# A hybrid RWKV-7 and MoBA layer: alternating the two halves of the array in small products, with TensorE in program order

## The chip, the cores and the metric

The kernel runs on one core of one Trainium2 chip. The metric is device time in microseconds (us) of one execution. Before the change the median of three runs is 842.22 us (840.99 to 842.25). All durations below come from one profiled execution of that kernel.

## The reference, cut to what matters

One decoder layer on 256 tokens of width 2048, in float32. The input is normalised, one product with `w_in` (2048 x 12416) feeds two token mixers and their gates, each mixer's result goes through a projection of its own, the two are merged by gates, and `w_out` closes the layer:

```
h = rms_norm(x, norm_w);  p = h @ w_in
y_a = rwkv7_mix(p_r, p_k, p_v, p_wd, p_ad, ...) * silu(z_a)
y_b = moba_attention(p_q, p_kq, p_vq, q_norm_w, k_norm_w) * silu(z_b)
merged = sigmoid(g_a) * (y_a @ w_proj_rwkv) + sigmoid(g_b) * (y_b @ w_proj_moba)
out = x + merged @ w_out
```

Both mixers have 16 heads of 64 features. The RWKV mixer is a recurrence over the tokens, which the kernel computes in blocks of 64 tokens: it needs the products of all keys with all queries of a block, an inverse of a triangular matrix of 32 x 32, and a state carried from block to block. With 256 tokens and blocks of 256 the MoBA mixer is plain causal attention: logits, softmax, values.

## The kernel before, in words

**Jobs.** The large products are cut into chunks of 512 columns (`chunk`, L240), and each chunk into jobs: half of a 1 MB load of weights, which ACT and DVE split into a high and a low part (`split_hi` L211, line 216; `split_lo` L218, line 222), so that three fast products stand for one exact one. A job is 24 matmuls of 256 columns (`mm_fm`, line 329) or 12 of 512 columns (`mm_tm`, lines 347 to 349). There are 258 jobs, numbered from 0. `run_jobs` (L253) emits `prep(i)`, the split of job i, then `run(i - 2)`: the matmuls of the job two before, the work on a finished chunk (`post`), and `pump()`. The parts of a split have three buffers each.

**Side work.** Everything else is written as generators. `pump()` (L199) takes one step of each generator in `urgent` and one step of the first one in `queue`; a step ends at a `yield`. A step may hold TensorE, DVE, ACT and GpSimd instructions. A stretch of side work on TensorE between two jobs is called a visit here. `drain(mark)` (L203) takes steps, one after the other, until a named generator is through; `with_need("m0", ...)` and `with_need("v1", ...)` (L1027, L1040) call it ahead of a chunk's post.

The features are handled in two groups of 512 (g = 0, 1), and in a tile of 128 partitions two heads lie one above the other (p = 0 in partitions 0 to 63, p = 1 in 64 to 127). For each group the steps are, in order:
- `rwkv_elem` (L405): low-rank products (lines 430, 431) into two PSUM tiles `pw` and `pa`, each read by ACT sigmoids (lines 432, 435); norms of the keys (line 467, ACT line 469, DVE lines 470 to 473, transposes at line 481).
- `rwkv_r` (L511): the key products, line 533, for each of 4 feature tiles `fi` and each half p a PSUM tile with 4 products of 64 x 128 by 64 x 128, then DVE line 536.
- `rwkv_mid` (L659): the inverse on DVE (lines 564, 567) alongside transposes (lines 620, 643), then a trip through DRAM (lines 571, 576) and the products at lines 593 and 601.
- `rwkv_v` (L680): twelve steps over 4 blocks: lines 670 and 677, ACT line 690; line 694, ACT line 697; line 704. These products already alternate p = 0, p = 1.
- `moba` (L808): six units, for p = 0 then p = 1 one unit u = 0 (4 heads, 128 queries by 128 keys) and two units u = 1, 2 (2 heads, 128 by 256). `logits` (lines 825, 831) is followed by DVE lines 836 to 839 and ACT exponentials (line 843); `normal` by DVE lines 848, 849; `turn` transposes four tiles (line 858) and ACT copies them; `pv` (lines 874, 876) multiplies by the values for one p at a time.
- Group norms (`group_norm`, L720, transposes at line 748) and the transposes of q and k (`qk_post`, L760, line 775, after DVE line 793) run as urgent generators.

**What sets the order.** The program is written with Tile and its scheduler (`schedule_with_timeline_sim=True`). Inside `tc.manual_schedule(engines=...)` the engines named keep the order in which the program emits their instructions; elsewhere the scheduler orders each engine's instructions by its own timing model, the earlier emitted ones first among those that it finds ready. Before the change only the start is ordered by hand (L294: jobs 0 to 3, on DVE, ACT and PE). From job 6 on (L306) all engines are ordered by the scheduler. The root mean square of x (`rms_x`, L158) is emitted in that second loop ahead of job 4: DVE line 159, ACT line 160, DVE line 161, then two TensorE transposes (line 164).

An f32 matmul appears in the trace as two MATMUL records, an f32r one (the main products) and a transpose as one.

Of the kernel before, what the change touches and what calls it, by code (L numbers as in the profile page):

```python
# [13 lines left out]
AF = mybir.ActivationFunctionType  # L14
# [22 lines left out]
def tile_hybrid_block(ctx: ExitStack, tc: tile.TileContext, x, pv, wdu, wau,  # L37
# [17 lines left out]
    def T(tag, shape, dt=F32, bufs=1):  # L55
        return sb.tile(shape, dt, tag=tag, name=nm(tag), bufs=bufs)
# [4 lines left out]
    def PSS():  # L61
        return psd.tile([P, 512], F32, tag="ps", name=nm("ps"))
# [95 lines left out]
    def rms_x():  # L158
        dve.tensor_reduce(rsx, ssx, AX.X, ALU.add)
        act.activation(rsx, rsx, AF.Sqrt, bias=epsr, scale=1.0 / D)  # L160
        dve.reciprocal(rsx, rsx)
        pt = PSS()
        for t in range(2):
            pe.transpose(pt[:, t * P:(t + 1) * P], rsx[:, t:t + 1].to_broadcast([P, P]), ident)
        dve.tensor_copy(rbc, pt[:, 0:S])
# [87 lines left out]
    def run_jobs(look):  # L253
        n = len(jobs)
        emitted = [0]

        def ensure(j):
            while emitted[0] <= j and emitted[0] < len(loads):
                emit_load(emitted[0])
                emitted[0] += 1  # L260

        def prep(i):
            jb = jobs[i]
            ensure(jb["ld"] + 1)
            jb["raw"] = loads[jb["ld"]]["raw"]
            if i >= KT // 2:
                split_hi(jb)
                split_lo(jb)
            elif i:
                split_hi(jb)  # L270
                scale_hi(i, 0)
                scale_hi(i, 1)
                split_lo(jb)
                scale_lo(i, 0)
                scale_lo(i, 1)
            else:
                for u in range(2):
                    split_hi(jb, u)
                    scale_hi(0, u)
                    split_lo(jb, u)  # L280
                    scale_lo(0, u)

        def run(i):
            jb = jobs[i]
            if jb["first"] and jb["pre"]:
                jb["pre"]()
            jb["mm"](jb)
            if jb["end"]:
                jb["post"](jb["st"])
            pump()  # L290


        wt = PSS()
        with tc.manual_schedule(engines=ordered):  # L294
            for _ in range(8):
                pe.transpose(wt[:, 0:P], ident, ident)
            for j, i, turns, sqs in ((None, 0, (0, 1), ()), (None, 1, (), ()), (0, 2, (2, 3), ()),
                                     (1, 3, (), ((0, 0), (1, 0))), (2, 4, (4, 5), ((0, 1), (1, 1))),
                                     (3, 5, (6, 7), ())):
                if j is not None:  # L300
                    run(j)
                turn_x(*turns)
                prep(i)
                for a in sqs:
                    square_x(*a)
        for i in range(6, n + look):  # L306
            if i < n:
                prep(i)
            if i == 6:
                rms_x()  # L310
            if i >= look:
                run(i - look)

    def mm_fm(mh, ml):
        def f(jb):
# [195 lines left out]
    def rwkv_r(g):  # L511
# [14 lines left out]
        r["rr"] = (rh, rl)  # L526
        yield
        for fi in range(4):
            for p in range(2):
                ps = PSS()  # L530
                sl = slice(64 * p, 64 * p + 64)
                for c in range(4):
                    pe.matmul(ps[:, c * P:(c + 1) * P],  # L533
                              bk[sl, fi, c].rearrange("p a t -> p (a t)"),
                              ar[sl, fi, c].rearrange("p a t -> p (a t)"), start=True, stop=True)
                dve.copy_predicated(
                    LL[p][:, fi].rearrange("p c a t -> p c (a t)"),
                    m2.rearrange("p a t -> p (a t)").rearrange("p (o t) -> p o t", o=1)
                    .to_broadcast([P, 4, P]),
                    ps.rearrange("p (c t) -> p c t", c=4))  # L540
            yield
        G = T("sg", [64, 32, 32])
        gd = dp.tile([4, 4, 4, 32, 32], F32, tag="gd", name=nm("gd"))
# [263 lines left out]

    def moba(g):  # L808
        q, k, v = M[g]["q"], M[g]["k"], M[g]["v"]
        s1 = T("cs", [P, 2, 2, S])  # L810
        smt = [T("sg", [P, 4, P]), s1[:, 0], s1[:, 1]]
        for ap in (smt[0], s1):
            pool.memset(ap, -1e30)
        yield
        us = [dict(p=p, u=u, nh=2 if u else 4, nk=S if u else P, sm=smt[u])
              for p in range(2) for u in range(3)]
        pts = {}
        prs = T("bk", [P, 4, 512])

        def logits(n, w):  # L820
            rows = slice(64 * w["p"], 64 * w["p"] + 64)
            ps = PSS()
            if w["u"] == 0:
                for fi in range(4):
                    pe.matmul(ps[:, fi * P:(fi + 1) * P], q[rows, fi, 0:P], k[rows, fi, 0:P],  # L825
                              start=True, stop=True)
                mask = mq[:, 1:2, :].to_broadcast([P, 4, P])
            else:
                for i in range(2):
                    fi = 2 * (w["u"] - 1) + i  # L830
                    pe.matmul(ps[:, i * S:(i + 1) * S], q[rows, fi, P:S], k[rows, fi, :],  # L831
                              start=True, stop=True)
                mask = mq.rearrange("p a t -> p (a t)").rearrange(
                    "p (o t) -> p o t", o=1).to_broadcast([P, 2, S])
            nh, nk, sm = w["nh"], w["nk"], w["sm"]
            dve.copy_predicated(sm, mask, ps.rearrange("p (f t) -> p f t", f=nh))
            mx = T("mx", [P, 4], bufs=2)
            dve.tensor_reduce(mx[:, 0:nh], sm, AX.X, ALU.max)
            dve.tensor_scalar(mx[:, 0:nh], mx[:, 0:nh], -0.125, None, ALU.mult)
            w["Pr"] = prs[:, n % 4, :].rearrange("p (a b) -> p a b", a=nh)  # L840
            w["sum"] = T("smx", [P, 4], bufs=2)
            for i in range(nh):
                act.activation(w["Pr"][:, i, :], sm[:, i, :], AF.Exp, scale=0.125,
                               bias=mx[:, i:i + 1], accum_out=w["sum"][:, i:i + 1])

        def normal(w):
            nh, nk = w["nh"], w["nk"]
            dve.reciprocal(w["sum"][:, 0:nh], w["sum"][:, 0:nh])
            dve.tensor_tensor(w["Pr"], w["Pr"], w["sum"][:, 0:nh].rearrange(
                "p (h o) -> p h o", o=1).to_broadcast([P, nh, nk]), ALU.mult)  # L850

        def turn(w):
            if w["u"] == 0:
                pts[w["p"]] = T("ar", [P, 4, 3, P])
            pt = pts[w["p"]]
            ps = PSS()
            for i in range(4):
                pe.transpose(ps[:, i * P:(i + 1) * P],  # L858
                             w["Pr"].rearrange("p a b -> p (a b)")[:, i * P:(i + 1) * P], ident)
            if w["u"] == 0:  # L860
                act.activation(pt[:, :, 0, :], ps.rearrange("p (f t) -> p f t", f=4), AF.Copy)
            else:
                f0 = 2 * (w["u"] - 1)
                act.activation(pt[:, f0:f0 + 2, 1:3, :],  # L864
                               ps.rearrange("p (f b t) -> p f b t", f=2, b=2), AF.Copy)

        def pv(p):
            rows = slice(64 * p, 64 * p + 64)
            pt = pts[p]
            po = [PSS() for _ in range(2)]  # L870
            for fi in range(4):
                o = po[fi // 2][rows, (fi % 2) * S:(fi % 2 + 1) * S]
                col = slice(fi * P + 64 * p, fi * P + 64 * p + 64)
                pe.matmul(o, v[:, 0, col], pt[:, fi, 0:2, :].rearrange("p a t -> p (a t)"),  # L874
                          start=True, stop=True, skip_group_check=True)
                pe.matmul(o[:, P:S], v[:, 1, col], pt[:, fi, 2, :], start=False, stop=True,
                          skip_group_check=True)
            for half in range(2):
                act.activation(oT[rows, 4 * g + 2 * half:4 * g + 2 * half + 2, :].rearrange(
                    "p f t -> p (f t)"), po[half][rows, :], AF.Copy)  # L880

        for n in range(9):
            if n in (5, 8):
                pv(0 if n == 5 else 1)
            if 2 <= n < 8:
                turn(us[n - 2])
            if 1 <= n < 7:
                normal(us[n - 1])
            if n < 6:
                logits(n, us[n])  # L890
            yield


# [153 lines left out]
        chunk(w_out, 512 * i, 512, KT, out_mm(cuts, out_done(i, sx)), lambda st: None,  # L1047
              pre=out_pre(i, sx))
    run_jobs(2)
    drain()  # L1050


_W = ["w_in", "w_proj_rwkv", "w_proj_moba", "w_out"]
# [39 lines left out]
```

## Time and profile before

| | |
|---|---|
| median of 3 runs | 842.22 us |
| profiled execution, its own time | 843.0 us |
| its span in the trace | 841.3 us |
| TensorE (PE) busy | 832.2 us, 99% |
| DVE busy | 554.3 us, 66% |
| ACT busy | 422.2 us, 50% |
| MATMUL records | 6738 |

The page of the profile gives busy times by engine and the chain of work that ended last. Matmuls are pipelined and their ends are modelled, so a record's duration is longer than the distance to the next; the number of records in a stretch says more than the share that is busy. A row of the timeline holds start, duration, engine, line, operation, tiles, shape and count; neighbours of one kind are merged.

### The profile page before, as it was taken

What the parts mean: (1) busy time and instruction counts of PE and PEld (TensorE: products, weight loads), DVE (VectorE), ACT (ScalarE), POOL (GpSimd) and SP (SyncE); (2) the same over time, 40 slices, a digit from 0 to 9 for tenths busy, and PEclk for the clock granted to TensorE, in tenths of its full rate; (3) what the DMA queues carried; (4) which work ended last, traced back from release to release, by engine and by line L of the source; (5) the groups of instructions that cost most, each with busy time, mean ns of one, the idle gap of its engine ahead of it and who ended that gap; (6) DMA issues with size and microseconds to landing.
All of it is one profiled execution on the core that took longest, in us unless ns stands there. A gap on an engine that the chain in (4) does not pass through costs nothing.

```text
span 841.3 us, 15850 instructions
## 1 busy us (share of the span) xinstructions
PE 832.2 (99%) x6738; PEld 771.0 (92%) x6738; DVE 554.3 (66%) x776; ACT 422.2 (50%) x568; POOL 29.0 (3%) x42
## 2 busy tenths in 40 slices
PE   8999999999999999999999999999999999999998
PEld 7999878899998788899999988999999999998887
DVE  5869958956569569749974579554455566664553
ACT  6785435444437585435444477544444444443342
POOL 5001100000000002000000000000000000000000
PEclk9999999999999999999999999999999999999999
DMA  8564555564434344646564323555656655556772
GB/s 302 176 195 156 178 160 164 179 196 152 136 117 151 110 141 150 195 139 195 199 204 147 106 97 121 191 188 187 195 197 201 198 164 190 198 167 213 231 245 98
DMA packets 83206, 145.78 MB, mean 173 GB/s; under 512 B 11568, under 2 KB 13872, under 8 KB 83136
## 3 DMA queue, kind: packets, MB, share of 16 engines
q1 hardware_dynamic: 71584, 138.55, 50.7%
q10 hardware_dynamic: 11520, 6.16, 2.7%
q8 instruction: 53, 0.87, 0.4%
q14 instruction: 17, 0.14, 0.0%
q0 software_dynamic: 32, 0.05, 0.0%
HBM read 141.61 MB, written 3.15 MB: 172 GB/s over the span
## 4 chain that ended last, share of the span: by engine, by line
PE 98%; DVE 1%; DMA 1%; issue 0%; SPq 0%; ACT 0%
PE pm L329 59%; PE pm L348 9%; PE pm L347 9%; PE pm L349 9%; PE ps L533 2%; PE ps L670 1%; PE ps L831 1%; PE ps L874 1%; PE ps L677 1%; PE ps L858 1%; DMA raw<-in_w_in_dram 1%; PE ps L694 1%; PE ps L825 1%; PE ps L601 0%; PE ps L593 0%; PE ps L704 0%
## 5 line engine op out<-in xcount | busy, mean ns | idle before, releaser
L216 ACT ACTIVATE hi<-raw 128x1024 fp32r<-128x1024 f32 (+1 forms) x259 | 273.1, 1056 | 350.5 <-PE pm L329 214.7
L222 DVE TENSOR_TENSOR lo<-raw,hi 128x1024 fp32r<-128x1024 f32 (+1 forms) x259 | 314.5, 1217 | 203.1 <-ACT hi L216 199.5
L329 PE MATMUL pm<-xh,hi 128*128 128x256 f32 x1168 | 327.3, 282 | 1.0 <-ACT xh L144 1.0
L329 PE MATMUL pm<-xh,lo 128*128 128x256 f32 x1168 | 324.3, 279 | 1.0 <-DVE lo L222 1.0
L329 PE MATMUL pm<-xl,hi 128*128 128x256 f32 x1168 | 324.3, 279 | 0.0
L329 PEld LDWEIGHTS pm<-xh,hi 128*128 128x128 f32 x1168 | 219.7, 189 | 4.7 <-ACT xh L144 1.4
L329 PEld LDWEIGHTS pm<-xh,lo 128*128 128x128 f32 x1168 | 219.9, 189 | 2.6 <-DVE lo L222 1.4
L329 PEld LDWEIGHTS pm<-xl,hi 128*128 128x128 f32 x1168 | 219.8, 189 | 0.6
L348 PE MATMUL pm<-lo,xh 128*128 128x512 f32 x192 | 76.3, 398 | 0.0
L349 PE MATMUL pm<-hi,xl 128*128 128x512 f32 x192 | 75.6, 394 | 0.0
L347 PE MATMUL pm<-hi,xh 128*128 128x512 f32 x192 | 73.5, 398 | 0.0
L348 PE MATMUL pm<-lo,mgh 128*128 128x512 f32 (+1 forms) x128 | 48.4, 378 | 0.0
L349 PE MATMUL pm<-hi,mgl 128*128 128x512 f32 (+1 forms) x128 | 48.0, 376 | 0.0
L347 PE MATMUL pm<-hi,mgh 128*128 128x512 f32 (+1 forms) x128 | 44.4, 377 | 0.0
L348 PEld LDWEIGHTS pm<-lo,xh 128*128 128x128 f32 x192 | 36.1, 188 | 8.3 <-issue 0.5
L349 PEld LDWEIGHTS pm<-hi,xl 128*128 128x128 f32 x192 | 36.1, 188 | 7.5 <-issue 0.2
L347 PEld LDWEIGHTS pm<-hi,xh 128*128 128x128 f32 x192 | 35.9, 188 | 7.6 <-ACT ar L864 0.2
L347 PEld LDWEIGHTS pm<-hi,mgh 128*128 128x128 f32 x128 | 24.0, 188 | 4.7
L349 PEld LDWEIGHTS pm<-hi,mgl 128*128 128x128 f32 x128 | 24.0, 188 | 4.7
L348 PEld LDWEIGHTS pm<-lo,mgh 128*128 128x128 f32 x128 | 24.0, 188 | 4.4
L564 DVE TENSOR_TENSOR tmp<-sg,kk 64x31 f32<-64x31 f32 (+15 forms) x62 | 20.5, 331 | 5.9 <-DMA sg<-gd 4.7
L329 PE MATMUL pm<-bk,hi 128*128 128x256 f32 x128 | 22.8, 281 | 0.0
(280 smaller groups left out, 1014.3 us busy)
## 6 DMA issues: line engine op xcount, KB each, us to landing
raw<-in_w_in_dram SPq DMA_DIRECT2D x94, 1024.0 KB, 5.1
raw<-in_w_out_dram SPq DMA_DIRECT2D x16, 1024.0 KB, 5.3
raw<-in_w_proj_moba_dram SPq DMA_DIRECT2D x8, 1024.0 KB, 5.1
raw<-in_w_proj_rwkv_dram SPq DMA_DIRECT2D x8, 1024.0 KB, 5.0
raw<-in_w_in_dram SPq DMA_DIRECT2D x5, 512.0 KB, 6.6
k<-in_x_dram ACTq DMA_DIRECT2D x4, 256.0 KB, 4.2
r<-in_x_dram ACTq DMA_DIRECT2D x4, 256.0 KB, 3.8
k<-in_x_dram SPq DMA_DIRECT2D x2, 256.0 KB, 5.1
```

Source lines behind the costliest of these rows:

```text
L216: act.activation(job["hi"][:, c], job["src"][:, c], AF.Copy)
L222: dve.tensor_tensor(job["lo"][:, c], job["src"][:, c], f32(job["hi"][:, c]), ALU.subtract)
L329: pe.matmul(o, (hi, hi, lo)[ps][:, i, cs], (mh, ml, mh)[ps](k), start=(k == 0 and fi % 2 == 0 and ps == 0), stop=(k == jb["last"] and ps = ...
L347: pe.matmul(o, sh[:, k, ts], hi[:, i, cs], start=(k == 0), stop=False)
L348: pe.matmul(o, sh[:, k, ts], lo[:, i, cs], start=False, stop=False)
L349: pe.matmul(o, sl[:, k, ts], hi[:, i, cs], start=False, stop=end)
L533: pe.matmul(ps[:, c * P:(c + 1) * P], bk[sl, fi, c].rearrange("p a t -> p (a t)"), ar[sl, fi, c].rearrange("p a t -> p (a t)"), start=True ...
L564: dve.tensor_tensor(tv, gcol.to_broadcast([64, nt, j + 1]), trow.to_broadcast([64, nt, j + 1]), ALU.mult)
L670: pe.matmul(ps[64 * p:64 * p + 64, c0 + 64 * fi:c0 + 64 * fi + 64], LL[p][:, fi, c, which, :], UV[:, c, p, fi, :], start=(fi == 0), stop=( ...
L677: pe.matmul(ps[sl, c0 + 64 * fi:c0 + 64 * fi + 64], ar[sl, fi, c, which, :], St[sl, fi, :], start=False, stop=True, skip_group_check=True)
L694: pe.matmul(ps[sl, cols], X64[sl, fi * 4 + c, :], Zs[sl, cols], start=True, stop=True)
L825: pe.matmul(ps[:, fi * P:(fi + 1) * P], q[rows, fi, 0:P], k[rows, fi, 0:P], start=True, stop=True)
```

## The change

1. `tc.manual_schedule(engines={PE})` is put around the whole second loop of `run_jobs`, and the last `drain()` moves into it. TensorE takes every instruction from job 4 on in program order; DVE, ACT and the queues are still ordered by the scheduler.
2. In the key products the two PSUM tiles of a feature tile are allocated together, and the matmuls alternate between the halves p = 0 and p = 1.
3. `moba` is rewritten. A unit covers both halves: 3 units instead of 6. The logits alternate between the halves (two PSUM tiles). The values are multiplied unit by unit in products of 128 columns, alternating between the halves of one PSUM tile, so 24 products of 128 columns replace 16 of 256 and 128; two copies to `oT` replace four. The steps of a group go from 9 to 14 after the one that fills the buffers: logits 0, logits 1, and for each unit `normal` of half 0, `normal` of half 1 with `turn` of half 0, `turn` of half 1 (with logits 2 in the first unit), `pv`.

```diff
+        with tc.manual_schedule(engines={mybir.EngineType.PE}):
+            for i in range(6, n + look):
+                if i < n:
+                    prep(i)
+                if i == 6:
+                    rms_x()
+                if i >= look:
+                    run(i - look)
+            drain()
...
+            pss = [PSS() for _ in range(2)]
+            for c in range(4):
+                for p in range(2):
+                    sl = slice(64 * p, 64 * p + 64)
+                    pe.matmul(pss[p][:, c * P:(c + 1) * P],
...
+        def logits(w):
+            u, nh, nk = w["u"], w["nh"], w["nk"]
+            pss = [PSS() for _ in range(2)]
+            for i in range(nh):
+                fi = i if u == 0 else 2 * (u - 1) + i
+                for p, rows in enumerate(halves):
+                    pe.matmul(pss[p][:, i * nk:(i + 1) * nk],
+                              q[rows, fi, 0:P] if u == 0 else q[rows, fi, P:S],
+                              k[rows, fi, 0:nk], start=True, stop=True)
...
+        def pv(w):
+            u = w["u"]
+            pt = pts[:, u % 2]
+            if u < 2:
+                po.append(PSS())
+            o = po[-1]
+            for i in range(4 if u == 0 else 2):
+                fi = i if u == 0 else 2 * (u - 1) + i
+                for b in range(1 if u == 0 else 2):
+                    for p, rows in enumerate(halves):
+                        col = slice(fi * P + 64 * p, fi * P + 64 * p + 64)
+                        pe.matmul(o[rows, fi * P:(fi + 1) * P], v[:, b, col],
+                                  pt[:, p, i if u == 0 else 2 * i + b, :],
+                                  start=(b == 0), stop=(b == (u > 0)), skip_group_check=True)
...
+        logits(us[0])
+        yield
+        logits(us[1])
+        yield
+        for n in range(3):
+            normal(us[n], 0)
+            yield
+            normal(us[n], 1)
+            turn(us[n], 0)
+            yield
+            turn(us[n], 1)
+            if n == 0:
+                logits(us[2])
+            yield
+            pv(us[n])
             yield
...
     run_jobs(2)
-    drain()
```

## Rows read from the trace of the kernel before

**Rows 1.** The page, busy time by engine.
```profile
PE 832.2 (99%) x6738; PEld 771.0 (92%) x6738; DVE 554.3 (66%) x776; ACT 422.2 (50%) x568; POOL 29.0 (3%) x42
```

**Rows 2.** Groups by line and form, PE: records, busy us, mean ns, idle before.
```profile
L533 PE MATMUL ps<-ar,bk 64*128 64x128 f32 x128 | 14.5, 288 | 0.0
L670 PE MATMUL ps<-UV,LL 128*64 128x64 f32 x256 | 11.9, 226 | 0.0
L874 PE MATMUL ps<-ar,vq 128*64 128x256 f32 x32 | 9.9, 392 | 0.0
L831 PE MATMUL ps<-kn,qn 64*128 64x256 f32 x32 | 9.0, 402 | 0.0
...
L876 PE MATMUL ps<-ar,vq 128*64 128x128 f32 x32 | 6.1, 272 | 0.0
...
L825 PE MATMUL ps<-kn,qn 64*128 64x128 f32 x32 | 4.6, 285 | 0.0
```

**Rows 3.** Timeline of PE: one visit each; the last in a 10 ns window.
```profile
112.58 1.71 PE L533 MATMUL ps<-ar,bk 64*128 64x128 f32 x16
...
248.81 1.16 PE L825 MATMUL ps<-kn,qn 64*128 64x128 f32 x8
...
202.20 0.27 PE L694 MATMUL ps<-Zs,X 64*64 64x64 f32 x2
```

**Rows 4.** Timeline of PE, ACT and DVE around the transposes of rms_x.
```profile
23.82 0.48 PE L329 MATMUL pm<-xh,hi 128*128 128x256 f32 x2
...
27.86 0.15 DVE L161 RECIPROCAL rsx<-rsx 128x2 f32<-128x2 f32 x1
...
30.86 0.38 PE L164 MATMUL ps<-ident,rsx 128*128 128x128 f32 x2
```

**Rows 5.** Timeline of PE and ACT in the first low-rank products, group 0.
```profile
49.81 0.28 PE L431 MATMUL ps<-xx,lora 128*128 128x256 f32 x1
...
53.44 0.28 PE L430 MATMUL ps<-xx,lora 128*128 128x256 f32 x1
...
50.73 1.28 ACT L435 ACT_TABLE_LOAD   x1
...
52.40 0.47 ACT L432 ACTIVATE sg<-ps,pv 128x256 f32<-128x256 f32 x1
```

**Rows 6.** Stretches, all engines: length, busy us and (records), clock, DMA.
```profile
8.00:12.00 4.00, 4.00 (x19) 4.00 (x20) 3.46 (x10) 2.69 (x6) 2.17 (x10) 1.00 1.02 373
...
410.00:440.00 30.00, 30.00 (x268) 30.00 (x267) 24.62 (x45) 12.81 (x14) 0.53 (x1) 1.00 0.68 211
```

**Rows 7.** Timeline: norms of the keys, group 0, and q/k work, group 1.
```profile
67.90 1.84 PE L467 MATMUL ps<-sel,bk 128*128 128x2 f32 x16
...
77.04 0.68 DVE L473 COPY bk<-n 128x1024 f32<-128x1024 f32 x1
...
318.16 1.84 PE L467 MATMUL ps<-sel,bk 128*128 128x2 f32 x16
...
333.85 1.27 DVE L793 TENSOR_TENSOR qkn<-pm,ssk 128x512 f32<-128x512 f32 x2
```

**Rows 8.** Groups by line and form, DVE: records, busy us, mean ns, idle before.
```profile
L222 DVE TENSOR_TENSOR lo<-raw,hi 128x1024 fp32r<-128x1024 f32 x257 | 313.1, 1221 | 202.9 <-ACT hi L216 199.3 <-PE pm L329 2.6
L849 DVE TENSOR_TENSOR bk<-bk,smx 128x512 f32<-128x512 f32 x12 | 8.3, 690 | 0.2
...
L836 DVE COPY_PREDICATED cs<-mq,ps 128x512 f32<-128x512 uint8 x8 | 5.9, 736 | 1.9 <-PE ps L831 1.9
```

**Rows 9.** Timeline around the trip through DRAM, group 1 (ACTq is ACT's queue).
```profile
392.85 0.60 PE L643 MATMUL ps<-ident,bk 128*128 128x128 f32 x4
...
435.31 2.17 ACTq L576 DMA_DIRECT2D cs<-td  x4
...
440.65 0.31 PE L593 MATMUL ps<-cs,LL 32*32 32x32 f32 x4
```

**Rows 10.** Timeline of ACT: a copy between two dependent visits.
```profile
210.15 0.39 ACT L690 ACTIVATE Zs<-ps 128x256 f32<-128x256 f32 x1 [0.29 <-PE ps L677]
```

More of the change, by code (lines that the diff above doesn't have):

```diff
@@ L305, in run_jobs @@
                     square_x(*a)
[L306 to L312, printed above, removed]
+        with tc.manual_schedule(engines={mybir.EngineType.PE}):
[7 more added lines that the diff above has]
+            drain()
     def mm_fm(mh, ml):
@@ L528, in rwkv_r @@
         for fi in range(4):
[L529 to L533, printed above, removed]
+            pss = [PSS() for _ in range(2)]
[3 more added lines that the diff above has]
+                    pe.matmul(pss[p][:, c * P:(c + 1) * P],
                               bk[sl, fi, c].rearrange("p a t -> p (a t)"),
                               ar[sl, fi, c].rearrange("p a t -> p (a t)"), start=True, stop=True)
+            for p in range(2):
                 dve.copy_predicated(
@@ L539, in rwkv_r @@
                     .to_broadcast([P, 4, P]),
-                    ps.rearrange("p (c t) -> p c t", c=4))
+                    pss[p].rearrange("p (c t) -> p c t", c=4))
             yield
@@ L809, in moba @@
         q, k, v = M[g]["q"], M[g]["k"], M[g]["v"]
-        s1 = T("cs", [P, 2, 2, S])
-        smt = [T("sg", [P, 4, P]), s1[:, 0], s1[:, 1]]
-        for ap in (smt[0], s1):
+        smt = [T(t, [P, 2, 512]) for t in ("sg", "cs")]
+        for ap in smt:
             pool.memset(ap, -1e30)
         yield
[L815 to L826, printed above, removed]
+        prs = T("bk", [P, 2, 2, 512])
@@ new lines, in moba @@
+        pts = T("ar", [P, 2, 2, 4, P])
+        us = [dict(u=u, nh=2 if u else 4, nk=S if u else P) for u in range(3)]
+        halves = [slice(0, 64), slice(64, 128)]
+        po = []
+        def logits(w):
[7 more added lines that the diff above has]
+                              k[rows, fi, 0:nk], start=True, stop=True)
+            if u == 0:
@@ L827, in logits @@
                 mask = mq[:, 1:2, :].to_broadcast([P, 4, P])
             else:
[L829 to L832, printed above, removed]
                 mask = mq.rearrange("p a t -> p (a t)").rearrange(
                     "p (o t) -> p o t", o=1).to_broadcast([P, 2, S])
-            nh, nk, sm = w["nh"], w["nk"], w["sm"]
-            dve.copy_predicated(sm, mask, ps.rearrange("p (f t) -> p f t", f=nh))
@@ L837, in logits @@
[L837 to L849, printed above, removed]
+            w["Pr"], w["sum"] = [], []
+            for p in range(2):
+                sm = smt[u > 0][:, p, :].rearrange("p (a b) -> p a b", a=nh)
+                dve.copy_predicated(sm, mask, pss[p].rearrange("p (f t) -> p f t", f=nh))
+                mx = T("mx", [P, 4], bufs=2)
+                dve.tensor_reduce(mx[:, 0:nh], sm, AX.X, ALU.max)
+                dve.tensor_scalar(mx[:, 0:nh], mx[:, 0:nh], -0.125, None, ALU.mult)
+                Pr = prs[:, u % 2, p, :].rearrange("p (a b) -> p a b", a=nh)
+                sums = T("smx", [P, 4], bufs=4)
+                for i in range(nh):
+                    act.activation(Pr[:, i, :], sm[:, i, :], AF.Exp, scale=0.125,
+                                   bias=mx[:, i:i + 1], accum_out=sums[:, i:i + 1])
+                w["Pr"].append(Pr)
+                w["sum"].append(sums)
@@ L850, in normal, with turn @@
+        def normal(w, p):
+            nh, nk, sums, Pr = w["nh"], w["nk"], w["sum"][p], w["Pr"][p]
+            dve.reciprocal(sums[:, 0:nh], sums[:, 0:nh])
+            dve.tensor_tensor(Pr, Pr, sums[:, 0:nh].rearrange(
                 "p (h o) -> p h o", o=1).to_broadcast([P, nh, nk]), ALU.mult)
[L852 to L855, printed above, removed]
+        def turn(w, p):
             ps = PSS()
@@ L858, in turn @@
                 pe.transpose(ps[:, i * P:(i + 1) * P],
[L859 to L890, printed above, removed]
+                             prs[:, w["u"] % 2, p, i * P:(i + 1) * P], ident)
+            act.activation(pts[:, w["u"] % 2, p].rearrange("p a t -> p (a t)"), ps, AF.Copy)
+        def pv(w):
[12 more added lines that the diff above has]
+                                  start=(b == 0), stop=(b == (u > 0)), skip_group_check=True)
+            if u != 1:
+                t = slice(0, P) if u == 0 else slice(P, S)
+                act.activation(oT[:, 4 * g:4 * g + 4, t], o.rearrange("p (f t) -> p f t", f=4),
+                               AF.Copy)
```

## The prediction

> **What bounds the kernel now.** I read the page first. TensorE is busy for 832.2 us of the 841.3 us span, DVE for 66% and ACT for 50% of it [rows 1]. So the time is TensorE's own, and only two things can move it: records taken out of its stream, and gaps put into it. The groups by line give the first. Beside the main products, the four families that the change rearranges hold 14.5 us (key products), 4.6 and 9.0 us (logits), 9.9 and 6.1 us (values), 44.1 us in all, and not one of these groups shows idle time before it [rows 2]: whenever a side product is not ready, the scheduler lets main products go ahead. That is the second thing, since the change forbids it.
>
> **The pairs: what is saved.** In the timeline one visit of the key products, 16 records with the halves one behind the other, lasts 1.71 us; a visit of 8 records of the same 128 columns, all in one half, lasts 1.16 us [rows 3]. Products that alternate between halves exist already: a window of 10 ns holds the starts of two records of line 694 [rows 3], and line 670, whose halves share all 128 rows and differ in columns alone, takes 11.9 us for 256 records, 46 ns each [rows 2]. So I price two alternating records as one.
> - Key products: 8 visits of 8 pairs, each like the 8-record visit: 8 x 1.16 = 9.3 us instead of 14.5. Saved: 5.2.
> - First logits: 2 visits of 8 pairs, 2 x 1.16 = 2.3 instead of 4.6. Saved: 2.3.
> - Longer logits: 32 records now take 9.0 us, 1.13 for four; afterwards 4 visits of 4 pairs, 4.5. Saved: 4.5.
> - Values: now 9.9 + 6.1 = 16.0 us. Afterwards 24 products a group, 96 records of 128 columns in all, 48 pairs in 6 visits of 8: 6 x 1.16 = 7.0. Saved: 9.0.
>
> Together 21.0 us. The transposes of line 858 stay as many. DVE and ACT do the same work, less two copies to `oT` a group; that is off the path and costs nothing, as long as TensorE does not stand waiting for these engines.
>
> The Trainium skill speaks against the last item. "TensorE: Matmul & The Clock Gate", in "The mechanism" under its Part 3, says that a weight load runs beside a matmul in flight only if the two use different rows. By that rule the values, whose halves use the same rows, would save nothing. Line 670 has that shape and shows 46 ns a record [rows 2]; the trace disagrees, and I follow it.
>
> **The order: what is added.** Now TensorE stops wherever a product is not ready at its place in the program, and every job queued behind it stops too. For each place I compare when TensorE would get there with when its input was there in this trace. A job's place is counted in main records of 112 ns (268 in 30 us [rows 6]), 24 to a job, 2.7 us.
> - (a) The transposes of `rms_x` are emitted ahead of job 4. TensorE starts job 4 at 23.82; the reciprocal that they read ends at 27.86 + 0.15 = 28.01; the scheduler ran them at 30.86, with jobs in between [rows 4]. DVE and ACT have the two splits before it in program order, so it won't come sooner. Wait: 4.2.
> - (b) In the low-rank products the second matmul pair of a step writes the PSUM tile that a sigmoid is still reading. The first four records go at 49.8; ACT loads a table (1.28 us from 50.73) and ends the sigmoid of `pw` at 52.87; the next pair on that tile ran at 53.44 [rows 5]. In program order the sigmoid of `pw` comes first and would end near 52.5, so 2.5 us of waiting from about 50.0; the second step needs no table: one sigmoid and its handover, 0.8. 3.3 a group, 6.6 in all.
> - (c) Line 481, group 0: TensorE is there two jobs after the visit that ends at 67.90 + 1.84, at 75.1; its input (line 473) ends at 77.72 [rows 7], 2.6 later. The sigmoids of (b) now end earlier relative to TensorE, so I take half, 1.3; ends 0 and 2.6.
> - (d) Transposes of k, group 1: four jobs and one short visit after 320.0, so 331.8; line 793 ends at 335.12 [rows 7]: 3.3. The RWKV steps of group 1 begin a job later after the change, which frees DVE there; with half a microsecond for the same place of q in group 0, I take 2.0; ends 0 and 4.
> - (e) MoBA. From the first logits to the first transposes TensorE needs three jobs and two visits, 8.1 + 2.3 = 10.4 us. DVE has in that time four masked copies of 0.74 and four maxima (an estimate: the size of line 849, 0.69), three splits of 1.22, one normalisation of 0.69 [rows 8] and the group norm, four such passes: 5.7 + 3.7 + 0.7 + 2.8 = 12.9. Wait: 2.5. At the next transposes DVE also has the post of the V chunk, six or seven passes: 2.3 more. The drain of `m0` at the end of the Q chunk (job 81) falls into the now longer generator, and runs its last three steps without jobs between: 0.9 for one copy. In group 1 there is no V post: 2.5. Together 8.2. No row shows these waits, so the ends are 2 (the scheduler finds room for DVE) and 14.
> - (f) Line 593, group 1: 15 jobs after 393.2, so 433.5. The reads from DRAM that it needs are still being issued until 435.31 + 2.17 = 437.48, and it ran at 440.65 [rows 9]. Wait between 4.0 and 7.1; I take 6.0. This chain hangs on DVE and the trip through DRAM, which the change does not shorten. In group 0 the same place is just reached in time.
> - (g) The drain of `v1` (job 137) now runs three dependent visits in a row instead of two. One turn from TensorE through ACT and back is 0.29 + 0.39 us [rows 10] and a handover back, near 0.9. Two turns: 2.0; ends 1 and 3.
> - (h) After standing still, TensorE may restart slowly. From 8 to 12 us, after the start's gaps, it began 19 records in 4 us where later 36 fit [rows 6]; once slow costs 1.9 us. (a) and (f) are the longest waits; no row shows a restart after a wait of that length. I take one, 1.9; ends 0 and 5.
>
> Sum of the waits: 4.2 + 6.6 + 1.3 + 2.0 + 8.2 + 6.0 + 2.0 + 1.9 = 32.2. Lowest ends (b 4): 15. Highest (b 8, f 7): 48. What would be late next after each is the same stream: no second engine bounds it.
>
> 32.2 - 21.0 = 11.2 us more. The profiled execution took 843.0, so 854.2; the median lies 0.8 below that execution: 853.4.
>
> "What's actually happening", in Part 1 of the same page of the Trainium skill, says that inactivity lowers TensorE's clock and activity raises it. The slow records fit its lower level, 1.2 GHz, though the profile's granted clock reads 1.00 there [rows 6]. It would put term (h) at its upper end.
>
> **The rivals.**
> 1. *The waits are mostly absorbed; faster.* The scheduler remakes DVE's and ACT's order around a TensorE that now stops, and each stop lets them catch up, so that (c), (d), (e) and half of (f) vanish. For: DVE is idle for a third of the span. Against: (a), (b) and (g) are chains, not load. Left: 4.2 + 5 + 3 + 1.5 = 13.7, minus 21.0: 835. It decides where the waits sum to under 21. Chance 0.21.
> 2. *Column halves don't pair.* The skill's rule above, as a mechanism here: the values stay at 16.0 us, the gain is 12.0, the time 862. Against it stands line 670. Chance 0.06.
> 3. *The order was the program's already.* Then the manual schedule changes nothing, the waits are nil: 821. Against: lines 164 and 481 ran later than their places [rows 4, 7]. Chance 0.04.
> 4. *Waits feed on each other.* Each long wait is followed by a slow restart, and in MoBA each late step makes the next late: upper ends of (e), (h), so 5.8 + 3.1 more and some of (b) and (f): 864. Chance 0.05.
>
> **How the numbers follow.** The forecast, that waits exceed the pairs, has 0.64. About 0.2%, 1.7 us, is what a measurement of this kernel can tell from no change; 0.06 of the forecast's lower tail and 0.02 of rival 1's upper tail lie within it. Faster: 0.19 + 0.04 = 0.23. Slower: 0.58 + 0.06 + 0.05 = 0.69. Same: 0.08. The range goes from 836 (lowest ends of the waits with the full gain: 842.2 + 15 - 21) to 866 (rival 2, rival 4 and the waits' sum at 45). It leaves out rival 3, the lower half of rival 1 and the far end of the waits. The forecast's own range is 841 to 864.
>
> **What would show it.** Each group of the four families should fall to the busy time above, pairs of starts within 10 ns; line 874 should not be much above 7 us. PE should have some 25 to 35 us less busy than its span, where 9 are now; in the waits, PE's idle time should stand ahead of line 164 (4 us, for line 161), line 430 (for ACT line 432), line 858 (for DVE line 849) and line 593 (for the DMA). The forecast falls if these idle times sum to less than 21, or if the values' records start one by one.

## The result, and the profile after

The changed kernel takes 873.67 us (872.32 to 875.85, four runs) beside 841.61 us (840.28 to 842.25, four runs) of the kernel before on the same chip: a ratio of 1.0386, interval 1.0357 to 1.0414. The direction was forecast; the size was not: 853.4 was said, and 873.67 lies 8 us above the upper end of the range. The profiled execution took 872.32 us, its span is 870.6.

Lines of the kernel after are a few higher than before: 333 and 351 to 353 are the main products, 434 the low-rank ones, 485 the transposes of the key norms, 538 the key products, 599 the products behind the trip through DRAM, 676 the first products of the recurrence, 781 the transposes of q and k, 835 the logits, 867 MoBA's transposes, 882 the values.

The page of the kernel after, busy time by engine, and the granted clock in 40 slices:

```profile
PE 829.4 (95%) x6770; PEld 772.0 (89%) x6770; DVE 553.1 (64%) x776; ACT 416.9 (48%) x563; POOL 29.7 (3%) x42
...
PEclk9999999999999999999997999999999999999999
```

Beside [rows 1] this splits the loss in two. TensorE's idle time, span less busy, went from 841.3 - 832.2 = 9.1 to 870.6 - 829.4 = 41.2 us: 32.1 more. Its busy time went from 832.2 to 829.4: only 2.8 less, although 20 us of work had gone.

That the work had gone is in the groups by line and form of the kernel after (records, busy us and mean ns, idle time before):

```profile
L676 PE MATMUL ps<-UV,LL 128*64 128x64 f32 x256 | 11.0, 226 | 0.6 <-ACT UV L703 0.5
L538 PE MATMUL ps<-ar,bk 64*128 64x128 f32 x128 | 9.3, 285 | 0.0
...
L882 PE MATMUL ps<-ar,vq 128*64 128x128 f32 x96 | 7.8, 280 | 2.2 <-ACT ar L869 2.1
...
L835 PE MATMUL ps<-kn,qn 64*128 64x256 f32 x32 | 4.5, 402 | 0.0
...
L835 PE MATMUL ps<-kn,qn 64*128 64x128 f32 x32 | 2.3, 285 | 0.0
```

The four families hold 9.3 + 7.8 + 4.5 + 2.3 = 23.9 us where they held 44.1 [rows 2]: 20.2 less, 21.0 forecast.

The waits of TensorE in the kernel after (what waits, for what: us in all, times, longest):

```profile
PE ps L599 <- DMA cs<-td: 8.7, 2, 8.3
PE ps L434 <- ACT sg L436: 7.1, 4, 2.5
PE ps L781 <- DVE qkn L799: 4.7, 2, 4.5
PE ps L164 <- DVE rsx L161: 4.1, 1, 4.1
...
PE ps L485 <- DVE bk L477: 2.6, 2, 2.1
PE ps L882 <- ACT ar L869: 2.1, 3, 0.8
PE pm L333 <- DVE lo L222: 2.0, 2, 1.4
PE ps L867 <- DVE bk L861: 1.1, 1, 1.1
PE ps L867 <- ACT v L374: 0.8, 1, 0.8
PE ps L676 <- ACT UV L703: 0.5, 1, 0.5
```

Before the change none of the groups of [rows 2] had idle time before it. All but line 333 are places that the prediction named, and the sum without that line, 31.7 us, is near its 30.3 (terms a to g).

What was foreseen only once, as term (h), is in the stretches of the kernel after that follow such waits (length, PE busy us and records, granted clock, DMA):

```profile
28.00:30.00 2.00, 2.00 (x14) 0.64 1.03 311
30.00:32.00 2.00, 2.00 (x11) 0.51 0.00 1
32.00:34.00 2.00, 2.00 (x19) 1.00 0.00 0
...
88.00:90.00 2.00, 2.00 (x12) 0.50 0.74 174
...
146.00:148.00 2.00, 2.00 (x9) 0.50 0.00 0
206.00:208.00 2.00, 2.00 (x12) 0.51 0.69 165
...
464.00:468.00 4.00, 4.00 (x42) 0.50 0.00 0
```

Behind the waits of lines 164, 485, 781 and 599 the granted clock is at its lower level, 0.5 (1.2 GHz), and TensorE, busy all the time, begins 11 records in 2 us where 19 fit just afterwards. Before, the mean granted clock was 1.000; now it is 0.986, which is 0.014 x 870.6 = 12 us of full speed, some of it within the waits. The stretches are not the same in each execution (the row from 206 us has no counterpart in the second profile of this kernel, shown further on).

### The profile page after: what moved, and what is told of

Same layout as the page of the kernel before. It is cut to its first block, busy times and chain, and to the rows that moved or that the text cites. A ratio compares the mean times of both kernels' runs of the same rounds, so it can differ in the third digit from the quotient of the medians.

```text
span 870.6 us, 15898 instructions
## 1 busy us (share of the span) xinstructions
PE 829.4 (95%) x6770; PEld 772.0 (89%) x6770; DVE 553.1 (64%) x776; ACT 416.9 (48%) x563; POOL 29.7 (3%) x42
## 4 chain that ended last, share of the span: by engine, by line
PE 78%; DVE 8%; ACT 5%; DMA 5%; issue 2%; ACTq 0%; SPq 0%; DVEq 0%
PE pm L333 48%; PE pm L351 8%; PE pm L352 7%; PE pm L353 7%; DVE lo L222 3%; ACT hi L216 2%; DMA raw<-in_w_in_dram 2%; DMA cs<-td 1%; DMA td<-kk 1%; PE ps L676 1%; PE ps L538 1%; PE ps L683 1%; DMA sg<-gd 1%; PE ps L882 1%; ACT bk L853 1%
## 5 line engine op out<-in xcount | busy, mean ns | idle before, releaser
L333 PE MATMUL pm<-xh,hi 128*128 128x256 f32 x1168 | 333.3, 286 | 0.5 <-ACT xh L144 0.5
L333 PE MATMUL pm<-xh,lo 128*128 128x256 f32 x1168 | 327.7, 282 | 2.0 <-DVE lo L222 2.0
L333 PEld LDWEIGHTS pm<-xh,hi 128*128 128x128 f32 x1168 | 222.8, 191 | 4.8 <-issue 1.5
L333 PEld LDWEIGHTS pm<-xh,lo 128*128 128x128 f32 x1168 | 224.3, 193 | 2.4 <-DVE lo L222 2.4
L333 PEld LDWEIGHTS pm<-xl,hi 128*128 128x128 f32 x1168 | 222.6, 191 | 0.1
L351 PE MATMUL pm<-hi,xh 128*128 128x512 f32 x192 | 77.4, 403 | 0.0
L351 PE MATMUL pm<-hi,mgh 128*128 128x512 f32 (+1 forms) x128 | 48.4, 378 | 0.0
```

The lines of the kernel that those rows point to most:

```text
L333: pe.matmul(o, (hi, hi, lo)[ps][:, i, cs], (mh, ml, mh)[ps](k), start=(k == 0 and fi % 2 == 0 and ps == 0), stop=(k == jb["last"] and ps = ...
L351: pe.matmul(o, sh[:, k, ts], hi[:, i, cs], start=(k == 0), stop=False)
```

## The experiments

Theory A: the pairs gain what was forecast, and the order costs more than its waits, since slow work follows them. The rivals differ from run to run and stand with each expectation.

**Each part alone.** In the first kernel the manual schedule is taken out again, the pairs stay:

```diff
-        with tc.manual_schedule(engines={mybir.EngineType.PE}):
             for i in range(6, n + look):
...
         drain()
```

> The changed kernel with the scheduler's order on TensorE again (as before the change); the alternating halves and the rewritten MoBA stay. Theory A (the pairs save about 20 us, the program order adds about 50 us of waits and slow restarts): 822 us, at most 828 if the scheduler takes some pairs apart; TensorE never idle after the start. Rival B (the pairs or the rewritten MoBA save little, so the order costs less): 835 us or more.

In the second the kernel before gets the manual schedule and nothing else:

```diff
+        with tc.manual_schedule(engines={mybir.EngineType.PE}):
             for i in range(6, n + look):
...
+            drain()
```

> The kernel before with program order on TensorE alone; no alternating halves, the old MoBA. Theory A: the waits at the places that the change left as they were (rms_x 4 us, low-rank products 9, line 481 3, line 775 6, line 593 10) are all there, with 7 us of slow restarts, and the old MoBA, whose steps follow closer, waits longer than the new one's 6 us: 885 us, between 878 and 905. Rival B: 855 us, the waits being mostly those of the rewritten MoBA.

Measured: the pairs alone 830.94 us (830.17 to 834.87), ratio 0.9881, interval 0.9855 to 0.9908: faster than both kernels, than the one before by 1.2%. The order alone 893.11 us (892.07 to 895.7), ratio 1.0621, interval 1.0598 to 1.0644: in theory A's range, and rival B falls. The pages, pairs alone and then order alone:

```profile
PE 817.0 (99%) x6770; PEld 759.4 (92%) x6770; DVE 549.9 (66%) x776; ACT 420.5 (51%) x566; POOL 29.4 (4%) x42
```

```profile
PE 846.9 (95%) x6738; PEld 784.6 (88%) x6738; DVE 554.6 (62%) x776; ACT 423.6 (48%) x569; POOL 28.7 (3%) x42
```

The order alone adds 34.3 us of idle time (890.3 - 846.9 = 43.4, less 9.1) and also 14.7 us of busy time, with not one record more (6738 in both). Within the order the pairs take off 893.1 - 873.7 = 19.4 us, the forecast 21.0; but 2.2 us of this is idle time (43.4 against 41.2), since the waits are not the same in the two. Without the order they take off 10.5 (841.44 - 830.94), a miss for the 822 us of theory A. The groups of the pairs alone say where a part of the rest stayed:

```profile
L537 PE MATMUL ps<-ar,bk 64*128 64x128 f32 x128 | 10.8, 290 | 0.0
L881 PE MATMUL ps<-ar,vq 128*64 128x128 f32 x96 | 8.7, 282 | 0.0
...
L834 PE MATMUL ps<-kn,qn 64*128 64x256 f32 x32 | 5.7, 402 | 0.0
...
L834 PE MATMUL ps<-kn,qn 64*128 64x128 f32 x32 | 2.3, 285 | 0.0
```

27.5 us instead of 23.9: the scheduler sets main products between the halves and takes some pairs apart (the 64 key-product records of group 0 lie in stretches of 14, 8, 4, 6, 16 and 16, in the kernel after in four of 16). Another 3.1 us is idle time (829.2 - 817.0 = 12.2, less 9.1). The other few are not placed. The alternating halves and the rewritten `moba` were not run apart.

**The pairs held.** The pairs alone, with a manual schedule around each block of key products, logits and values, so that the halves must alternate (the key products at a high priority too):

```diff
+            with tc.high_priority(), tc.manual_schedule(engines={mybir.EngineType.PE}):
                 for c in range(4):
                     for p in range(2):
...
+            with tc.manual_schedule(engines={mybir.EngineType.PE}):
                 for i in range(nh):
```

> Only the pairs: the scheduler keeps its freedom everywhere else, and within each block of key products, logits and values the two halves must alternate as written. Theory A (the pairs that the scheduler took apart in the kernel without the order cost it 3.6 us of TensorE's busy time: 27.5 us in the four families against 23.9 with the order): 827 to 830 us, families 24 to 25 us. Rival B (a block that must alternate makes the scheduler wait for its second tile): 831 to 836 us.

Measured: 836.26 us (834.9 to 838.08), ratio 0.9927, interval 0.9905 to 0.9949. Theory A fell, and the time is that of rival B. The families come down only to 26.8 us (key products 10.1, logits 5.2 and 2.8, values 8.7) and the busy time goes up, from 817.0 to 822.3. Rival B's reason, waiting, is not shown: idle time is 13.0 us (835.3 - 822.3) beside 12.2. What the added busy time is stays open. Here the scheduler's free choice is better than the half order.

**One wait at a time.** First the row factors (a): `rms_x` is emitted three jobs later. Then the low-rank products (b): both feature tiles' products come ahead of the sigmoids.

```diff
-                if i == 6:
+                if i == 9:
                     rms_x()
```

> The changed kernel with rms_x emitted three jobs later (ahead of job 7). Theory A: the wait of 4.4 us ahead of job 4 and the slow restart behind it (1.5 us) go, and nothing later moves: 867.8 us. Rival C (the wait only moves, since DVE and ACT used the pause to get ahead, which they now lack further on): 872 us or more, with longer waits at the next places.

```diff
             for i in range(2):
                 fi = 2 * half + i
-                col = 4 * g + fi
...
+            for i in range(2):
+                fi = 2 * half + i
+                col = 4 * g + fi
                 act.activation(sg[:, fi, :, 1:65],
```

> The changed kernel with the sigmoids of a step emitted behind both of its feature tiles, so that no matmul writes a PSUM tile that a sigmoid is reading. Theory A: the waits of lines 430 and 431 (8.9 us with their visits) go: 864.8 us. Rival C (they move to the next place, the norms of the keys): 870 us or more.

Measured: 855.68 us (854.44 to 859.52) and 855.32 us (852.74 to 857.13): 18 us less than the changed kernel for each, two to three times what theory A expected, and rival C fell too. Each wait was gone from its list, the other stayed. So some 10 us were unexplained, and the changed kernel was run again, and both edits together.

> The changed kernel once more, unchanged, beside the kernels below on one chip. Theory A (the 18 us that each of the two single-wait kernels gained belongs to those waits and to what follows them): 872 to 876 us again, TensorE idle 41 us and its busy time 829 us as in the first profile. Rival B (some of the 18 us is a pace that differs from one profiled program or chip to the next, whatever the waits): below 869 us, or the same time with a busy time of 820 to 825 us.

> The changed kernel with both waits taken away at once: the transposes of the row factors three jobs later, and the sigmoids behind both feature tiles. Theory A (each wait costs its own idle time, 7 to 8 us, and its own slow work after it, 8 to 10 us): the two gains of 18 us add up, 836 to 841 us, TensorE idle 26 to 28 us. Rival B (8 to 10 us of the two gains are one common thing that either edit brings back): 844 to 851 us.

Measured: the changed kernel again 873.14 us (867.05 to 875.2), with a busy time of 824.1 us in its profile, so the second form of rival B; both edits 856.62 us (853.0 to 859.5), no better than one, and above the ranges of theory A and rival B alike. A part of what the two gains share is a pace of the main products. The products of a long plain stretch in four profiles (the changed kernel, its repeat, both edits, and the row factors alone):

```profile
570.00:610.00 40.00, 40.00 (x342) 1.00 0.59 189
```

```profile
570.00:610.00 40.00, 40.00 (x356) 1.00 0.61 199
```

```profile
570.00:610.00 40.00, 40.00 (x342) 1.00 0.56 185
```

```profile
570.00:610.00 40.00, 40.00 (x355) 1.00 0.57 186
```

At the same granted clock, without a gap, the same products run at one of two paces, 356 or 342 records in 40 us (113.3 or 117.8 ns from start to start). Two executions of one program differ in it, 865.3 and 870.6 us of span: of the 5.3 us, 4.2 arise between the starts of the main products number 3,000 and 4,000 (115.1 and 119.3 us apart), where 20 records of lines 867 and 882 are all the side work that is left (in the kernel before, with none left, 113.3). The profile of both edits had the slow pace, those of the single edits the quick one; the pace of the executions that were not profiled is not known. Ahead of that stretch the gains come nearer to adding up: main product 2,600 of 5,280 starts at 487.3 us in the repeat, 476.7 and 479.0 with one edit, 472.4 with both, so 10.6, 8.3 and 14.9 us earlier, where 18.9 would be the sum. The idle times agree: 41.2 in the repeat (865.3 - 824.1), 33.3 and 34.1 with one edit, 30.5 with both. With the row factors late the q and k transposes (line 781) waited 1.7 us (3.6 in the repeat, 4.7 in its first profile), which neither the second edit (4.4) nor both together (4.3) show. By these starts (b) costs 7.0 us of idle time and 1.3 behind it; (a) 4.1 of idle time and, both taken together, 2 to 3 behind it. What stands behind the waits is an estimate, since the stretches at the lower clock differ from one execution to the next.

**Idle turned into work.** Transposes of the identity, overwritten afterwards, ahead of three of the waits:

```diff
         pt = PSS()
+        for _ in range(24):
+            pe.transpose(pt[:, 0:P], ident, ident)
...
         pbt = [PSS() for _ in range(2)]
+        if g == 1:
+            for _ in range(50):
+                pe.transpose(pbt[0][:, 0:P], ident, ident)
...
+                if key == "q" and g == 0 and half == 0:
+                    for _ in range(26):
+                        pe.transpose(ps[:, 0:P], ident, ident)
```

> The changed kernel with idle turned into work and nothing else: 24 transposes of the identity ahead of the two of the row factors, 50 ahead of the correction products of the second group, 26 ahead of the first query transposes, all into the tile that is then overwritten; they run in the waits of 4.1, 8.3 and 4.5 us and take some 11 us by the 0.11 us of one such transpose. Theory A (a wait costs more than its length, because TensorE's clock is at its lower level during and after it): the granted clock no longer falls at these three places, idle 41 falls to 29 to 31 us, and the time to 862 to 869 us although work was added. Rival B (only the length of the waits counts): 872 to 876 us.

Measured: 868.08 us (864.98 to 871.05), 5.1 less than the repeat, with 100 transposes more. The two profiled executions, both of the quick pace, differ by 2.1 us (865.3 and 863.2 of span). Stretches as above:

```profile
28.00:30.00 2.00, 2.00 (x19) 1.00 1.07 318
30.00:32.00 2.00, 2.00 (x19) 1.00 0.05 16
...
88.00:90.00 2.00, 2.00 (x12) 0.59 0.90 232
...
146.00:148.00 2.00, 2.00 (x12) 1.00 0.00 0
...
464.00:468.00 4.00, 4.00 (x32) 0.64 0.02 4
```

At two of the three filled places, the row factors and the q transposes, the clock stays at 1.00, and 38 records begin between 28 and 32 us where 25 did. At the third, the correction products, 2.5 us of waiting were left behind the 50 transposes (8.0 in all in the repeat), and the clock still falls, to 0.64 from 464 to 468 us; so it does behind line 485, which was not filled. Idle time is 31.5 us (863.2 - 831.7). The transposes are busy for 2.8 + 5.6 + 3.0 = 11.4 us, but the busy time rose by 7.6 over the repeat's 824.1: 3.8 us of slow work went. Theory A holds for the clock at two places of three, and at the weak end of its range for the time.

**The price of a wait by itself.** Five holds in plain products of the changed kernel:

```diff
+        def hold(n):
+            t = T("tmp", [P, 256], bufs=2)
+            p0 = PSS()
+            pe.transpose(p0[:, 0:P], ident, ident)
+            act.activation(t[:, 0:P], p0[:, 0:P], AF.Copy)
+            for _ in range(n):
+                pool.tensor_tensor(t[:, 0:P], t[:, 0:P], t[:, 0:P], ALU.mult)
+            p1 = PSS()
+            pe.transpose(p1[:, 0:P], t[:, 0:P], ident)
```

> What a wait costs beyond its length, measured by itself: in the stretch of plain products near the gates the changed kernel gets five holds, eight jobs apart, each a transpose that waits for a copy on ScalarE and 0, 2, 4, 8 or 16 small products on GpSimd of the transpose before it; their results are not used. Theory A (a long wait brings TensorE's clock to its lower level and the products after it run slowly for a while): the shortest holds cost their length and under 0.4 us more, those of some 3 us and more cost their length and 1.2 to 2 us, with records 210 instead of 115 ns apart behind them and the granted clock at its lower level there. Rival B (a wait costs its length): under 0.4 us more for every one.

Measured: 905.46 us in one run. The timeline of TensorE around the fourth hold (start, duration, in brackets the idle time before):

```profile
603.76 0.27 PE L286 MATMUL ps<-ident 128*128 128x128 f32 x1
609.82 0.48 PE L291 MATMUL ps<-ident,tmp 128*128 128x128 f32 x1 [5.79 <-POOL tmp L289]
609.95 0.56 PE L345 MATMUL pm<-xh,hi 128*128 128x256 f32 x1
610.31 0.41 PE L345 MATMUL pm<-xl,hi 128*128 128x256 f32 x1
610.52 0.41 PE L345 MATMUL pm<-xh,lo 128*128 128x256 f32 x1
```

Behind the hold the starts lie 213 ns apart instead of 113, for 23 records: 2.6 us. Counted in the same way, the second hold (3.4 us from its first to its last transpose) cost 1.4 us behind it, the third (4.4) 1.7, the fourth (6.1) 2.6, the fifth (9.9) 2.4, the last two more than theory A's 2; the first (1.4), which fell among small products, none. Stretches behind the third hold, whose last transpose starts at 580.18, and around the fourth:

```profile
580.00:581.00 1.00, 0.81 (x7) 1.00 0.01 4
581.00:582.00 1.00, 1.00 (x7) 0.57 0.00 0
...
604.00:609.00 5.00, 0.04 (x1) 0.94 0.65 210
609.00:610.00 1.00, 0.18 (x2) 0.50 0.00 0
610.00:615.00 5.00, 5.00 (x24) 0.50 0.00 0
615.00:620.00 5.00, 5.00 (x44) 0.97 0.27 57
```

The clock explains the slow records, and rival B falls. Behind the third hold the first seven records still came at the full pace, and the clock fell while TensorE was working again; behind the fourth it had fallen before.

**All long waits covered.** Both edits, and besides the first q transposes two jobs later, line 485 one job later, line 599 of group 1 three jobs later:

```diff
-            yield
-            yield
-            yield
+            for _ in range(3 if g else 5):
+                yield
...
-        for _ in range(5):
+        for _ in range(5 + 3 * g):
             yield
```

> The changed kernel with its order and every long wait covered by more jobs: the row factors three jobs later and the sigmoids behind both feature tiles (as in the kernel with both, 856.6 us), and besides the first query transposes two jobs later, the transposes of the key norms one job later, the correction products of the second group three jobs later (two steps of vector work alone are joined to make room). Theory A (the order costs what its waits cost, 4.3 and 2.3 and 7.9 us there, and 1 to 2 us of slow work after each): 838 to 844 us, TensorE idle 16 to 19 us. Rival B (the later steps run out of jobs to cover them, and the wait comes back at the deadlines of the first attention and of the second group's recurrence): 848 us or more, with new rows of waits there.

Measured: 851.16 us (846.62 to 855.3), ratio 1.0104, interval 1.0088 to 1.0121. Main product 2,600 starts at 461.4 us, with the kernel before (459.9) but 10 us behind the pairs alone (451.3): up to there what is left of the order's cost takes all that the pairs gave. New waits stand in the list, as rival B has it:

```profile
PE pm L352 <- DVE lo L222: 3.6, 3, 2.8
...
PE pm L333 <- DVE lo L222: 2.2, 2, 1.7
...
PE ps L702 <- ACT Zs L698: 1.9, 1, 1.9
```

Line 702 stands in the recurrence of group 1, whose last eleven groups of products now run without a main product between them (483.2 to 495.4 us; in the kernel after the last five); idle time is still 25.4 us (853.6 - 828.2), and the profiled run, the slowest of the five, had the slow pace.

## Why the prediction was right in direction and wrong in size

- **The pairs.** 20.2 us in the groups against 21.0, and 19.4 by the time with and without them inside the order. Right, column halves included: the values' 96 records take 7.8 us, 7.0 forecast, where the mechanism of rival 2 left them at 16.0. The rule on weight loads of the Trainium skill ("TensorE: Matmul & The Clock Gate", "The mechanism") does not hold for these halves: by the prediction's reading of it nothing would have been saved.
- **The waits (a) to (g).** 30.3 us forecast; TensorE's idle time grew by 32.1. By the terms: (a) 4.2, measured 4.1; (b) 6.6, 7.1; (c) 1.3, 2.6, the upper end; (e) 8.2, measured 2.1 + 1.1 + 0.8 = 4.0, too high; (f) 6.0, measured 8.7, above its upper end of 7; (g) 2.0, 0.5 at line 676. So the sum came out right in part by luck: (e) and (g) were 5.7 too high, (c), (d) and (f) together 6.7 too low. Rival 1, that the waits are mostly absorbed, fell. Two more us, TensorE waiting for a split (line 333 for line 222; 1.0 before the change), had no term.
- **(d)** was in the wrong place: 2.0 was said, mostly for k of group 1; 4.7 was measured, nearly all at q of group 0, to which the prediction gave half a microsecond. The timeline of DVE and of ACT's queue there shows why:

```profile
137.24 0.49 ACTq L555 DMA_DIRECT2D sg<-gd  x1
...
138.41 0.36 DVE L797 TENSOR_SCALAR ssq<-ssq,rsx 128x8 f32<-128x8 f32 x2
...
143.21 0.18 DVE L570 TENSOR_TENSOR tmp<-sg,kk 64x31 f32<-64x31 f32 x1 [4.43 <-DMA sg<-gd]
143.32 1.27 DVE L799 TENSOR_TENSOR qkn<-pm,ssq 128x512 f32<-128x512 f32 x2
144.11 0.14 PEld L781 LDWEIGHTS ps<-ident,qkn 128*128 128x128 f32 x1 [4.89 <-issue]
```

  The first operation of the inverse (line 570) stands ahead of the q norm in DVE's queue and waits for a read from DRAM; line 799 stands behind it though its inputs are there, line 781 behind that, and in the fixed order everything behind line 781. A transfer off the path got on it through two queues.
- **(h), the slow restart, is the step that failed.** It took one restart of 1.9 us, with an upper end of 5, since "no row shows a restart after a wait of that length". The five stretches of the kernel after at the lower clock, which begin at 28.6, 86.6, 144.6, 206.1 and 458.6 us, show together what it was (their length, PE busy):

```profile
sum 23.90, PE 20.32; mean PE 4.06
```

  TensorE worked there for 20.3 us, in the repeat for 20.0, in the kernel before for none. As a record takes 213 ns instead of 113 at that clock, about half of it is lost: some 10 us (an estimate from these figures) where 1.9 stood. In both profiles each of the three longest waits was followed by such a stretch, some of those near 2 us were, and the holds price one at 1.4 to 2.6 us. Slower side products are in it (line 599 took 5.8 us, before 4.2).
- **What the busy time adds up to.** With all else as forecast it would have fallen by 21.0 - 1.9 = 19.1; it fell by 2.8, in the repeat by 8.1 (832.2 - 824.1). Of the 16.3 us between, some 8 are the restarts, 0.8 the pairs, and 4.2 the pace, by which the two profiled executions of the changed kernel differ and which no term covered. Some 3 us are not placed; 1.2 of them are in line 434 (5.2 us for its 16 records, as line 430 before 4.0), at a granted clock of 1.00 around both its groups. The order alone adds 14.7 us of busy time to the same records, a part of it by the slow pace (339 records from 570 to 610 us).
- The rule of the Trainium skill that the prediction cited ("What's actually happening" in Part 1 of the same page), that inactivity lowers the clock, agrees with the granted clock of 0.50 behind the fourth hold. The prediction kept it out of its sum, with the remark that at the start of the kernel the granted clock reads 1.00 [rows 6].

Rival 4, with a chance of 0.05 and 864 us, had in its first half the mechanism that came true, a slow restart behind each long wait, and sized it too low (5.0 us). Its second half, that in MoBA each late step makes the next late, did not come true: (e) fell short of its term. Rival 3, that the order was the program's already, fell with the order alone (893 us).

## What to carry to other kernels

An order that is right for a few small products need not be forced on the engine: here the pairs gave 10.5 us when they were only emitted in that order and the scheduler was free, 6.5 (842.72 - 836.26) when the order was held within their blocks, and the kernel lost 32 when the whole engine was ordered for their sake. When an engine that is never idle is put into program order, list every place where its input comes later than its turn, and price each as its length plus a restart at the lower clock, 1.4 to 2.6 us for the longer ones here. Look also one queue further: a wait on another engine that cost nothing before becomes the ordered engine's own.

## What the runs showed of the hardware that was not expected

- The granted clock can fall after the wait is over: behind the third hold (4.4 us) seven records came at full pace, then sixteen 213 ns apart.
- The same short wait is followed by a fall in one execution of a program and not in the next. Behind 2.1 us at line 485 the clock was 0.50 from 88 to 90 us in the first profile of the changed kernel, and 1.00 from 88 to 92 in the second; behind 2.3 us at line 434 it stayed at 1.00 from 48 to 64 in the first, and was 0.57 from 58 to 62 in the second.
- Gapless products of one form, at a granted clock of 1.00, run at one of two paces, 113.3 or 117.8 ns apart, for 120 us and more at a time. Two executions of the same program differed in it, and both paces stand in one execution too: in the kernel before, the starts lie 118 ns apart around 521.5 us and 113.3 from 570 to 610. What sets it stays open; it makes spans of the changed kernel uncertain by some 4 us, more than the 0.2% that the prediction took for the limit.
- Behind 64 records of small products of 32 x 32 (line 599, group 0), with a wait of only 0.38 us among them, the clock fell too (0.51 from 206 to 208 us); in the kernel before it reads 1.000 throughout, and in the repeat 1.00 from 200 to 212. Why it fell there was not tried.
